# A two-layer decoder trunk: feed-forward up products all token-major, gated result transposed after, weights split 1024 columns at a time

## The chip, the cores and the metric

The kernel runs on one core of a Trainium2 chip. The metric is the device time of one execution in microseconds (us). Engines are called as the profile calls them: PE (matrix products and transposes), DVE, ACT and POOL (elementwise work), SP (it only issues the big DMAs). Each engine runs its own instructions strictly in order.

## What is computed

Two layers of a decoder trunk on 256 tokens of width 1024. Layer 0 mixes tokens by multi-scale causal pooling, layer 1 by differential attention; both have a memory cross-attention beside the mixer and a half-step gated feed-forward network (FFN) before and after it, so there are four FFNs.

```python
def swiglu(h, w_up, w_down):
    gate, up = jnp.split(h @ w_up, 2, axis=-1)          # w_up 1024 x 5632, w_down 2816 x 1024
    return (jax.nn.silu(gate) * up) @ w_down
...
    mem_n = rmsnorm(mem, mem_norm_g)
    for i in range(DEPTH):                               # DEPTH = 2
        kv = mem_n @ mem_w_kv[i]
        x = x + 0.5 * swiglu(rmsnorm(x, norm_g[i, 0]), ffn_w_up[i, 0], ffn_w_down[i, 0])
        h = rmsnorm(x, norm_g[i, 1])
        mix = pool_layer(...) if i == 0 else diff_layer(...)   # on h, with keys and values from kv
        x = x + mix
        x = x + 0.5 * swiglu(rmsnorm(x, norm_g[i, 2]), ffn_w_up[i, 1], ffn_w_down[i, 1])
    return rmsnorm(x, final_norm_g)
```

## The kernel before

**Numbers in two parts.** Every operand of a product is held as the sum of two float32r tiles, `hi` and `lo`; a product is three matmuls (hi·hi, hi·lo, lo·hi, lines 231 to 233). Weights come as pieces of 128x2048 floats: SP loads a piece into one of three raw buffers (`RB`), ACT casts it to `hi` (L205), DVE subtracts to get `lo` (L208), in steps of `SPLIT` = 512 columns, into one of four pairs of buffers (`WB`). A raw buffer is free when its last `lo` is done. Operands made on the way are split the same way: a cast on ACT (`gh`, L220), then a subtraction on DVE (`gl`, L226).

**An FFN** works through 11 chunks of 256 hidden features (`ffn`, `NJ`). For a chunk it needs two pieces of up weights (gate and up columns) and one of down weights. After up product j the down product of an earlier chunk follows, which adds to four PSUM banks `acc`. Up products come in two forms. *Token-major* (`proj_tok`): the x columns are stationary and 512 weight columns move, 24 matmuls 128x512 per token tile t, two tiles. The gated result g then has tokens on partitions and is turned by PE transposes (L237, tile tr), 2 per token tile, cast to `gh` and subtracted to `gl`. *Feature-major* (`proj_wide`, L377, L379, L376): 128 weight columns are stationary, 8 matmuls of 512 and 8 of 256 columns per column tile, four column tiles a chunk; the result already lies as `gh` and `gl` need it, and `gate_columns` and `up_columns` do the rest on ACT and DVE. The first FFN does its first 3 chunks token-major, the others their first one; the other 38 chunks are feature-major. These need the norm's factor along the free axis, which `row_rstd` (L258) makes with four small matmuls (128x128 each in the profile), once per FFN.

**Closing a stage** (`close`): for a token tile, x is transposed in two halves of four transposes each, and for each half ACT makes four 128x128 `xT` hi parts with the gain (L222) and DVE four lo parts (L228), straight from PSUM.

**The order** of PE, ACT, DVE and SP is laid down while the program is built: `Flow` keeps a model clock, the products advance it, and chains of dependent steps (splitting a piece, gating a chunk, one attention head) are put between them when their model time comes. `finish` forces a chain's remaining steps in at once. `Weights` keeps the queue of pieces and issues a load as soon as a raw buffer counts as free. Special entries of the queue are `x` (its load goes to x itself, no raw buffer), `cols` and `mem` (the memory, split and normalised once, planned at j = 6 of the first FFN) and `final`. In the pool mixer `diff_consts` loads 64-wide constants `lp` by SP (L787), POOL multiplies them (`pr`), DVE sums (`dots`, L795), ACT takes exp (`ex`).

Of the kernel before, what the change touches and what calls it, by code (L numbers as in the profile page):

```python
# [35 lines left out]
SPLIT = 512  # L36
PACE = 0.0016
HURRY = 0.0016
AHEAD = 1
WB = 4  # L40
RB = 3
T2K = 8
ORDERED = {mybir.EngineType.PE, mybir.EngineType.Activation, mybir.EngineType.DVE, mybir.EngineType.SP}
# [7 lines left out]
# Spacing of the steps of a chain, in microseconds.  # L51
# [3 lines left out]
GATE = (1.1, 0.5, 0.25, 1.2, 0.05)  # L55
# [47 lines left out]
class Weights:  # L103
    """Pieces of the weights in the order of their use: loaded ahead, split ahead, handed out, released."""

    def __init__(self, flow, load, run):
        self.flow, self.load, self.run = flow, load, run
        self.queue, self.raw, self.done = [], [], {}
        self.started = self.live = 0
        self.running = False  # L110

    def pump(self):
        while len(self.raw) < min(len(self.queue), self.started + RB):
            self.raw.append(self.load(*self.queue[len(self.raw)]))
        if self.running or self.started == len(self.queue):
            return
        if isinstance(self.queue[self.started][0], tuple):
            if self.live == WB:
                return
            self.live += 1  # L120
        self.running = True
        self.flow.add(self.next())

    def next(self):
        key, src = self.queue[self.started]
        self.done[key] = yield from self.run(key, self.raw[self.started])
        self.started += 1
        self.running = False
        self.pump()
# [12 lines left out]
def trunk(ctx, tc, I, out):  # L142
# [8 lines left out]
    ps_tr = ctx.enter_context(tc.tile_pool(name="ps_tr", bufs=2, space=PSUM))  # L151
# [14 lines left out]

    def tr_bank():
        return ps_tr.tile([P, 512], F32, tag="tr", name=nm("tr"))

    def raw_tile():  # L170
        return wp.tile([P, PIECE], F32, tag="raw", name=nm("raw"), bufs=RB)

# [13 lines left out]
    def load(key, src):  # L186
# [4 lines left out]
        raw = raw_tile()  # L191
# [4 lines left out]
    def split_piece(key, raw):  # L196
# [5 lines left out]
        for s in range(0, PIECE + SPLIT, SPLIT):  # L202
            if s < PIECE:
                sl = slice(s, s + SPLIT)
                nc.scalar.copy(hi[:, sl], raw[:, sl])  # L205
            if s:
                sl = slice(s - SPLIT, s)
                nc.vector.tensor_sub(lo[:, sl], raw[:, sl], hi[:, sl].bitcast(F32))  # L208
            yield (PACE if len(W.done) >= AHEAD else HURRY) * SPLIT
        return hi, lo  # L210

    W = Weights(F, load, split_piece)
# [17 lines left out]
    def mm3(o, lh, ll, rh, rl, start, stop):  # L230
        nc.tensor.matmul(o, lh, rh, start=start, stop=False)  # L231
        nc.tensor.matmul(o, lh, rl, start=False, stop=False)  # L232
        nc.tensor.matmul(o, ll, rh, start=False, stop=stop)  # L233
# [20 lines left out]
    def row_rstd(rstd):  # L254
        """rstd of the tokens, along the free axis of every partition."""
# [20 lines left out]
    def columns(name):  # L276
        """Feature-major operand, K tile by K tile: both parts, and the two side by side."""
# [15 lines left out]
    def close(t, gain0):  # L293
# [6 lines left out]
        def parts(h):  # L300
            for k in range(4 * h, 4 * h + 4):
                yield xT[0][:, k, cols(t)], xT[1][:, k, cols(t)], b[h][:, cols(k % 4)], gcol[:, gain0 + k:gain0 + k + 1]

        def hi(h):
            for th, tl, src, g in parts(h):
                split_hi(th, src, g)

        def lo(h):
            for th, tl, src, g in parts(h):
                split_lo(tl, th, src, g)  # L310
# [4 lines left out]
        hi(0)  # L315
# [4 lines left out]
        hi(1)  # L320
# [23 lines left out]
    def proj_tok(hx, pcs, t, bank=mm_bank):  # L344
        """[128 tokens, 512] = h @ w; w in two pieces of four K tiles."""
# [11 lines left out]
    def proj_feat(hx, pcs, c):  # L357
        """[128 features, 256 tokens] for column tile c of the pieces."""
# [9 lines left out]
    def proj_wide(hx, pcs, c):  # L368
        """The same as two halves of a bank, to be added: the weights' first part meets both parts at once."""
        F.finish(*ready)  # L370
        o = mm_bank()
        for kk in range(KT):
            wh, wl = [v[:, kk % 4, cols(c)] for v in pcs[kk // 4]]
            last = kk == KT - 1
            if last:
                nc.tensor.matmul(o[:, 0:SEQ], wl, hx[0][:, kk, :], start=False, stop=False)  # L376
            nc.tensor.matmul(o, wh, hx[2][:, kk, :], start=kk == 0, stop=last)  # L377
            if not last:
                nc.tensor.matmul(o[:, 0:SEQ], wl, hx[0][:, kk, :], start=False, stop=False)  # L379
# [669 lines left out]
```

## Time and profile before

| | |
|---|---|
| time, median of 3 runs | 1035.28 us (1034.5 to 1036.14) |
| span of the profiled execution | 1033.5 us |
| PE busy | 1022.4 us, 99% of the span |
| DVE busy | 739.6 us, 72% |
| ACT busy | 610.4 us, 59% |
| weights and inputs read | 186.3 MB, 181 GB/s over the span |
| one raw piece, issue to landing | 4.8 us (median, up weights) |

The page gives the busy time of each engine, the span in 40 slices and the chain of work that ended last. The span runs from the first to the last profiled instruction; the median time is 1.8 us above it.

### The profile page before, as it was taken

What the parts mean: (1) busy time and instruction counts of PE and PEld (TensorE: products, weight loads), DVE (VectorE), ACT (ScalarE), POOL (GpSimd) and SP (SyncE); (2) the same over time, 40 slices, a digit from 0 to 9 for tenths busy, and PEclk for the clock granted to TensorE, in tenths of its full rate; (3) what the DMA queues carried; (4) which work ended last, traced back from release to release, by engine and by line L of the source; (5) the groups of instructions that cost most, each with busy time, mean ns of one, the idle gap of its engine ahead of it and who ended that gap; (6) DMA issues with size and microseconds to landing.
All of it is one profiled execution on the core that took longest, in us unless ns stands there. A gap on an engine that the chain in (4) does not pass through costs nothing.

```text
span 1033.5 us, 15028 instructions
## 1 busy us (share of the span) xinstructions
PE 1022.4 (99%) x5624; PEld 882.0 (85%) x5624; DVE 739.6 (72%) x1533; ACT 610.4 (59%) x1357; POOL 55.8 (5%) x125
## 2 busy tenths in 40 slices
PE   8999999999999999999999999999999999999997
PEld 7888888899888888888888888889998888888886
DVE  5767887756767677777777777756877867777675
ACT  5655755765666555556655565654766666555553
POOL 0000520100000000000000000010211000000000
PEclk9999999999999999999999999999999999999999
DMA  8754745535544555544554545446334544455541
GB/s 300 286 189 163 267 181 204 201 130 188 182 140 168 192 199 193 200 170 163 204 202 165 204 163 204 169 157 237 120 134 142 185 158 168 164 203 178 195 178 41
DMA packets 27993, 188.31 MB, mean 182 GB/s; under 512 B 3216, under 2 KB 3472, under 8 KB 5904
## 3 DMA queue, kind: packets, MB, share of 16 engines
q1 hardware_dynamic: 27632, 186.82, 49.7%
q8 instruction: 44, 0.72, 0.3%
q10 hardware_dynamic: 288, 0.52, 0.1%
q14 instruction: 29, 0.24, 0.1%
HBM read 186.29 MB, written 1.05 MB: 181 GB/s over the span
## 4 chain that ended last, share of the span: by engine, by line
PE 95%; DVE 2%; ACT 1%; DMA 1%; POOL 0%; SPq 0%; issue 0%; POOLq 0%; ACTq 0%
PE mm L377 28%; PE mm L379 12%; PE acc L231 10%; PE acc L233 10%; PE acc L232 10%; PE mm L231 6%; PE mm L233 6%; PE mm L232 6%; PE mm L376 2%; PE tr L237 1%; DMA raw<-in_ffn_w_up 1%; DVE lo L208 1%; ACT ds L841 1%; PE acc L822 0%; PE tr L232 0%; PE tr L233 0%
## 5 line engine op out<-in xcount | busy, mean ns | idle before, releaser
L208 DVE TENSOR_TENSOR lo<-raw,hi 128x512 fp32r<-128x512 f32 x684 | 440.7, 688 | 43.0 <-ACT hi L205 42.7
L377 PE MATMUL mm<-xT,hi 128*128 128x512 f32 x1216 | 424.2, 398 | 0.0
L205 ACT CAST hi<-raw 128x512 fp32r<-128x512 f32 x684 | 385.1, 618 | 26.9 <-PE mm L232 14.2
L379 PE MATMUL mm<-xT,lo 128*128 128x256 f32 x1064 | 298.5, 281 | 0.0
L377 PEld LDWEIGHTS mm<-xT,hi 128*128 128x128 f32 x1216 | 220.8, 188 | 42.4
L379 PEld LDWEIGHTS mm<-xT,lo 128*128 128x128 f32 x1064 | 201.0, 189 | 6.4
L231 PE MATMUL acc<-hi,gh 128*128 128x512 f32 x352 | 138.1, 392 | 0.0
L233 PE MATMUL acc<-hi,gl 128*128 128x512 f32 x352 | 137.1, 389 | 0.0
L232 PE MATMUL acc<-lo,gh 128*128 128x512 f32 x352 | 137.0, 389 | 0.0
L385 DVE TENSOR_TENSOR g<-g,mm 128x256 f32<-128x256 f32 x76 | 32.0, 421 | 80.6 <-ACT g L384 80.4
L384 ACT COPY s<-mm 128x256 f32<-128x256 f32 x76 | 28.3, 372 | 98.7 <-PE mm L377 98.7
L232 PEld LDWEIGHTS acc<-lo,gh 128*128 128x128 f32 x352 | 66.2, 188 | 13.9
L233 PEld LDWEIGHTS acc<-hi,gl 128*128 128x128 f32 x352 | 66.1, 188 | 14.0
L231 PEld LDWEIGHTS acc<-hi,gh 128*128 128x128 f32 x352 | 66.1, 188 | 11.9
L385 DVE TENSOR_TENSOR s<-s,mm 128x256 f32<-128x256 f32 x76 | 31.9, 420 | 57.8 <-ACT s L384 57.7
L439 ACT ACTIVATE s<-s 128x256 f32<-128x256 f32 x76 | 31.8, 418 | 68.5 <-DVE s L437 68.5
L220 ACT CAST gh<-g 128x256 fp32r<-128x256 f32 x76 | 30.9, 407 | 65.8 <-DVE g L445 65.8
L231 PE MATMUL mm<-xT,hi 128*128 128x256 f32 x192 | 55.9, 291 | 0.0
L233 PE MATMUL mm<-xT,lo 128*128 128x256 f32 x192 | 54.5, 284 | 0.0
L232 PE MATMUL mm<-xT,hi 128*128 128x256 f32 x192 | 54.3, 283 | 0.0
L231 PE MATMUL mm<-hi,xT 128*128 128x512 f32 x128 | 50.9, 398 | 0.0
L233 PE MATMUL mm<-hi,xT 128*128 128x512 f32 x128 | 50.0, 390 | 0.0
(190 smaller groups left out, 1364.1 us busy)
## 6 DMA issues: line engine op xcount, KB each, us to landing
raw<-in_ffn_w_up SPq DMA_DIRECT2D x86, 1024.0 KB, 4.8
raw<-in_ffn_w_down SPq DMA_DIRECT2D x44, 1024.0 KB, 5.0
raw<-in_diff_w_in SPq DMA_DIRECT2D x14, 1024.0 KB, 4.8
raw<-in_mem_w_kv SPq DMA_DIRECT2D x8, 1024.0 KB, 4.8
raw<-in_pool_w_in SPq DMA_DIRECT2D x6, 1024.0 KB, 4.9
raw<-in_pool_w_out SPq DMA_DIRECT2D x6, 1024.0 KB, 4.8
raw<-in_diff_w_out SPq DMA_DIRECT2D x6, 1024.0 KB, 4.7
raw<-in_ffn_w_up SPq DMA_DIRECT2D x8, 256.0 KB, 7.0
```

Source lines behind the costliest of these rows:

```text
L205: nc.scalar.copy(hi[:, sl], raw[:, sl])
L208: nc.vector.tensor_sub(lo[:, sl], raw[:, sl], hi[:, sl].bitcast(F32))
L220: nc.scalar.copy(hi, src)
L231: nc.tensor.matmul(o, lh, rh, start=start, stop=False)
L232: nc.tensor.matmul(o, lh, rl, start=False, stop=False)
L233: nc.tensor.matmul(o, ll, rh, start=False, stop=stop)
L376: nc.tensor.matmul(o[:, 0:SEQ], wl, hx[0][:, kk, :], start=False, stop=False)
L377: nc.tensor.matmul(o, wh, hx[2][:, kk, :], start=kk == 0, stop=last)
L379: nc.tensor.matmul(o[:, 0:SEQ], wl, hx[0][:, kk, :], start=False, stop=False)
L384: nc.scalar.copy(out, o[:, SEQ:2 * SEQ])
L385: nc.vector.tensor_add(out, out, o[:, 0:SEQ])
L439: nc.scalar.activation(s, s, AF.Silu)
```

## The change

1. `proj_wide`, `gate_columns`, `up_columns` and `row_rstd` inside the FFN are gone. Every chunk is token-major (`single`). The four transposes of a chunk stand together, after the second token tile's gating, in one bank (`one_bank("tr")`, a single buffer); `gh` and `gl` are then one 128x512 operation each. With `steps`, the down product lags one chunk (two in the first FFN), and the last step holds the last two (three) down products.
2. `SPLIT` is 1024: a piece is two casts on ACT, then two subtractions on DVE.
3. `close` copies each PSUM tile with its gain to SBUF (`xc`, four ACT operations per half as before), then casts all four 128x128 tiles in one ACT operation and subtracts in one DVE operation.
4. `Weights` counts free buffers by tag. The entry `x` takes no raw buffer but gives one back, so the count of free raw buffers is one too high from there on, and loads stand one piece earlier in SP's order.
5. `plan_ffn` adds `cols` and `mem` when `js[-1] == 5`, which holds for the up step and for the down step of chunk 5: the memory is loaded, split and normalised twice.
6. Further buffers' tags, `gh` and `gl` with three buffers; queries and keys in one tile.

```diff
-SPLIT = 512
-PACE = 0.0016
-HURRY = 0.0016
+SPLIT = 1024
+PACE = 1.2
+HURRY = 0.8
...
+        key, _, _, pre, post, frees = self.queue[self.started]
...
+        for tag in frees:
+            self.free[tag] += 1
...
         for s in range(0, PIECE, SPLIT):
+            nc.scalar.copy(hi[:, sl], raw[:, sl])
+            yield pace
+        for s in range(0, PIECE, SPLIT):
+            nc.vector.tensor_sub(lo[:, sl], raw[:, sl], hi[:, sl].bitcast(F32))
...
+        def scaled(h):
+            c = t2k("xc").rearrange("p (k n) -> p k n", k=4)
+            for k in range(4):
+                g = gain0 + 4 * h + k
+                nc.scalar.activation(c[:, k, :], b[h][:, cols(k)], AF.Copy, scale=gcol[:, g:g + 1])
+            b[h] = c
+            split_hi(xT[0][:, 4 * h:4 * h + 4, cols(t)], c)
 
         def lo(h):
-            for th, tl, src, g in parts(h):
-                split_lo(tl, th, src, g)
+            split_lo(xT[1][:, 4 * h:4 * h + 4, cols(t)], xT[0][:, 4 * h:4 * h + 4, cols(t)], b[h])
...
+            gts[j, t] = g
+            if t == 0:
+                return
+            yield SLACK
+            if begin and j in HOLD:
                 yield max(0, HOLD[j] - F.now)
+            F.finish(other)
+            part_tiles(j)
+            b = one_bank("tr")
+            for i in range(NT):
+                transposes(b[:, cols2(i)], gts[j, i], 2)
...
+        def single(j):
+            pcs = pieces(*[(layer, f, "up", j, q) for q in range(2)])
+            for t in range(NT):
+                o = proj_tok(xT, pcs, t, acc_bank if begin and j == 2 else mm_bank)
+                ids[j, t] = F.add(gated(j, t, o, ids.get((j, 0))))
+            ids[j, 0] = ids[j, 1]
             W.release(2)
...
+    def steps(begin):
+        lag = 2 if begin else 1
+        order = [("single", j) for j in range(lag - 1, lag)]
+        for j in range(lag, NJ):
+            order += [("single", j), ("down", j - lag)]
+        return order[:-1] + [("down", *range(NJ - 1 - lag, NJ))]
...
+            if begin and kind == "single" and js[0] == 2:
+                W.add("x", I["x"].rearrange("b (t p) d -> p (b t) d", p=P), "none")
+            if begin and js[-1] == 5:
+                W.add("cols", I["mem_cols"])
+                W.add("mem", I["mem"].rearrange("b (t p) d -> p (b t) d", p=P))
```

**Place one: the first FFN's start.** DVE, while the first three chunks are gated, before (acc and mm are products, tr the transposed chunks, rstd the norm's factor):

```order
L208 TENSOR_TENSOR lo_364<-raw_275,hi_363 128x512 x4
L416 SCALAR_TENSOR_TENSOR g_388<-acc_349,rstd_317,s_387 128x256
L208 TENSOR_TENSOR lo_402<-raw_311,hi_401 128x512 x2
L226 TENSOR_TENSOR gl_101<-tr_412,gh_100 128x512
L208 TENSOR_TENSOR lo_402<-raw_311,hi_401 128x512 x2
L226 TENSOR_TENSOR gl_253<-tr_432,gh_252 128x512
L260 COPY row_453<-tr_450 128x256
```

and now:

```order
L248 TENSOR_TENSOR lo_331<-raw_214,hi_330 128x1024 x2
L442 SCALAR_TENSOR_TENSOR g_370<-acc_333,rstd_276,s_375 128x256
L248 TENSOR_TENSOR lo_361<-raw_240,hi_360 128x1024 x2
L267 TENSOR_TENSOR gl_389<-tr_390,gh_388 128x512
L267 TENSOR_TENSOR gl_410<-tr_411,gh_409 128x512
L442 SCALAR_TENSOR_TENSOR g_421<-acc_371,rstd_292,s_432 128x256
```

Both `gl` of the first two chunks now follow two pairs of `lo` directly, and the transposes that the second one reads (tr_411) go into the same bank as the first one's (tr_390); before they had two banks.

**Place two: the pool mixer.** SP's order of loads before:

```order
L193 DMA raw_2008<-in_mem_w_kv 128x2048
L193 DMA raw_2098<-in_pool_w_in 128x2048
L787 DMA lp<-in_diff_lambda 128x256
L193 DMA raw_2148<-in_pool_w_in 128x2048
L193 DMA raw_2215<-in_mem_w_kv 128x2048
L193 DMA raw_2286<-in_mem_w_kv 128x2048
```

and now:

```order
L230 DMA raw_1684<-in_pool_w_in 128x2048
L230 DMA raw_1766<-in_pool_w_in 128x2048
L230 DMA raw_1795<-in_mem_w_kv 128x2048
L807 DMA lp<-in_diff_lambda 128x256
L230 DMA raw_1850<-in_mem_w_kv 128x2048
```

With three buffers in turn, a load takes over the buffer of the third load before it: the load ahead of `lp`, raw_2098, that of the pool groups' weights; now raw_1795 that of raw_1632. DVE at the same place, before (cat_lo are results of pool groups, pl their operands):

```order
L208 TENSOR_TENSOR lo_2153<-raw_2008,hi_2152 128x512
L226 TENSOR_TENSOR pl_2169<-acc_2170,ph_2168 128x512
L208 TENSOR_TENSOR lo_2153<-raw_2008,hi_2152 128x512 x2
L795 TENSOR_REDUCE dots<-pr 128x2
L226 TENSOR_TENSOR pl_2193<-acc_2194,ph_2192 128x512
L208 TENSOR_TENSOR lo_2223<-raw_2098,hi_2222 128x512 x2
```

and now:

```order
L269 SCALAR_TENSOR_TENSOR cat_lo_1615<-tr_1822,gcol,cat_hi_1614 128x256 x2
L267 TENSOR_TENSOR pl_1836<-acc_1837,ph_1835 128x512
L248 TENSOR_TENSOR lo_1799<-raw_1632,hi_1798 128x1024
L815 TENSOR_REDUCE dots<-pr 128x2
L267 TENSOR_TENSOR pl_1866<-acc_1867,ph_1865 128x512
L248 TENSOR_TENSOR lo_1863<-raw_1684,hi_1862 128x1024
```

Now the last reader of raw_1632, the second half of lo_1799, is the instruction just before `dots`, and `dots` needs `lp` by way of POOL; pl_1866, the operand of the last pool group, stands behind `dots`.

**Place three: the end of an FFN.** DVE at the end of the second FFN, before (x_res<-acc is the stage's result):

```order
L385 TENSOR_TENSOR s_4592<-s_4592,mm_4594 128x256
L437 TENSOR_TENSOR s_4592<-s_4592,row_3135 128x256
L385 TENSOR_TENSOR g_4593<-g_4593,mm_4624 128x256
L444 TENSOR_TENSOR g_4593<-g_4593,row_3135 128x256
L445 TENSOR_TENSOR g_4593<-g_4593,s_4592 128x256
L208 TENSOR_TENSOR lo_4646<-raw_4528,hi_4645 128x512
L226 TENSOR_TENSOR gl_4537<-g_4593,gh_4536 128x256
L208 TENSOR_TENSOR lo_4646<-raw_4528,hi_4645 128x512 x3
L291 SCALAR_TENSOR_TENSOR x_res<-acc_3258,x_res 128x512
```

and now:

```order
L267 TENSOR_TENSOR gl_3799<-tr_3800,gh_3798 128x512
L248 TENSOR_TENSOR lo_3790<-raw_3672,hi_3789 128x1024 x2
L442 SCALAR_TENSOR_TENSOR g_3815<-mm_3772,rstd_2604,s_3820 128x256
L442 SCALAR_TENSOR_TENSOR g_3847<-mm_3816,rstd_2693,s_3854 128x256
L248 TENSOR_TENSOR lo_3849<-raw_3708,hi_3848 128x1024 x2
L248 TENSOR_TENSOR lo_3872<-raw_3760,hi_3871 128x1024 x2
L267 TENSOR_TENSOR gl_3880<-tr_3881,gh_3879 128x512
L333 SCALAR_TENSOR_TENSOR x_res<-acc_2812,x_res 128x512
```

All four 1024-wide subtractions of the next two pieces now stand between the last chunk's g and its gl. PE there, before:

```order
L231 MATMUL acc_3259<-hi_4530,gh_4382 128x512
L232 MATMUL acc_3259<-lo_4531,gh_4382 128x512
L233 MATMUL acc_3259<-hi_4530,gl_4383 128x512
L231 MATMUL acc_3258<-hi_4573,gh_4536 128x512
L232 MATMUL acc_3258<-lo_4574,gh_4536 128x512
L233 MATMUL acc_3258<-hi_4573,gl_4537 128x512
```

and now:

```order
L273 MATMUL acc_2813<-hi_3762,gh_3798 128x512
L274 MATMUL acc_2813<-lo_3763,gh_3798 128x512
L275 MATMUL acc_2813<-hi_3762,gl_3799 128x512
L279 MATMUL tr_3881<-ident,g_3815 128x128 x2
L279 MATMUL tr_3881<-ident,g_3847 128x128 x2
L273 MATMUL acc_2812<-hi_3789,gh_3879 128x512
L274 MATMUL acc_2812<-lo_3790,gh_3879 128x512
L275 MATMUL acc_2812<-hi_3789,gl_3880 128x512
```

The last chunk's four transposes stand between the down product of the chunk before it and its own, whose first matmuls read gh_3879 and gl_3880; before, nothing stood there.

## Rows read from the trace of the kernel before

**Rows 1.** The page: engines' busy us (share, instructions); the last-ending chain by engine
```profile
PE 1022.4 (99%) x5624; PEld 882.0 (85%) x5624; DVE 739.6 (72%) x1533; ACT 610.4 (59%) x1357; POOL 55.8 (5%) x125
...
PE 95%; DVE 2%; ACT 1%; DMA 1%; POOL 0%; SPq 0%; issue 0%; POOLq 0%; ACTq 0%
```

**Rows 2.** By windows: us, five engines' busy (instructions), granted PEclk, DMA share, GB/s
```profile
340.64:357.36 16.72, 16.72 (x90) 14.32 (x89) 12.15 (x25) 9.47 (x20) 0.00 (x0) 1.00 0.51 190
...
1026.70:1030.00 3.30, 0.00 (x0) 0.00 (x0) 1.87 (x4) 1.51 (x4) 1.00 (x3) 1.00 0.00 0
1030.00:1031.00 1.00, 0.00 (x0) 0.00 (x0) 0.00 (x0) 0.03 (x1) 0.00 (x0) 0.52 0.33 121
```

**Rows 3.** Waits of PE: us in total, times, longest us
```profile
PE tr L237 <- DVE on L876: 1.2, 3, 0.6
```

**Rows 4.** Chain of waits, first FFN in steady state: start us, us, what
```profile
57.21 0.47 PE mm L377 x2
60.03 0.47 PE mm L377 x2
...
73.93 0.47 PE mm L377 x2
```

**Rows 5.** PE's timeline, pool mixer into second FFN: start us, us, what
```profile
304.06 0.39 PE L231 MATMUL mm<-hi,xT 128*128 128x512 f32 x1
...
308.14 0.60 PE L237 MATMUL tr<-ident,x_res 128*128 128x128 f32 x4
...
309.97 0.60 PE L237 MATMUL tr<-ident,x_res 128*128 128x128 f32 x4
310.33 0.48 PE L231 MATMUL mm<-hi,xT 128*128 128x512 f32 x1
```

**Rows 6.** Group by form: work, count | busy us, mean ns | idle
```profile
L237 PE MATMUL tr<-ident,x_res 128*128 128x128 f32 x80 | 12.0, 272 | 0.0
```

**Rows 7.** Timeline of ACT, DVE and PE, first FFN, chunks being gated
```profile
39.59 0.59 ACT L220 CAST gh<-tr 128x512 fp32r<-128x512 f32 x1 [1.29 <-PE tr L237]
...
37.80 0.48 DVE L416 SCALAR_TENSOR_TENSOR g<-acc,rstd,s 128x256 f32<-128x256 f32 x1
...
40.21 0.69 DVE L226 TENSOR_TENSOR gl<-tr,gh 128x512 fp32r<-128x512 f32 x1 [0.74 <-ACT gh L220]
...
41.46 0.60 PE L237 MATMUL tr<-ident,g 128*128 128x128 f32 x4
```

**Rows 8.** Timeline of SP, POOL, DVE and PE in the pool mixer
```profile
216.74 0.43 SPq L787 DMA_DIRECT2D lp<-in_diff_lambda  x1
...
221.52 0.65 POOL L793 TENSOR_TENSOR pr<-lp 128x64 f32<-128x64 f32 x2 [16.45 <-DMA lp<-in_diff_lambda]
...
226.41 1.28 DVE L208 TENSOR_TENSOR lo<-raw,hi 128x512 fp32r<-128x512 f32 x2
...
227.61 0.28 DVE L795 TENSOR_REDUCE dots<-pr 128x2 f32<-128x128 f32 x1
...
230.27 0.28 PE L231 MATMUL tr<-ph,hi 128*128 128x256 f32 x1
```

**Rows 9.** Timeline of ACT and DVE, pool mixer into second FFN, one closing half
```profile
308.78 1.14 ACT L222 ACTIVATE xT<-tr,gcol 128x128 fp32r<-128x128 f32 x4 [1.63 <-PE tr L237]
...
309.96 1.13 DVE L228 SCALAR_TENSOR_TENSOR xT<-tr,gcol,xT 128x128 fp32r<-128x128 f32 x4 [0.91 <-ACT xT L222]
```

**Rows 10.** Timeline of ACT, DVE and PE, end of the third FFN
```profile
664.74 0.40 PE L231 MATMUL acc<-hi,gh 128*128 128x512 f32 x1
...
665.33 1.28 ACT L398 ACT_TABLE_LOAD   x1
...
667.68 0.42 DVE L226 TENSOR_TENSOR gl<-g,gh 128x256 fp32r<-128x256 f32 x1 [0.39 <-ACT gh L220]
```

**Rows 11.** PE's timeline at the start: start us, us, work, idle before
```profile
6.43 0.80 PE L231 MATMUL acc<-hi,xT 128*128 128x512 f32 x1 [1.54 <-ACT xT L222]
...
9.59 0.40 PE L232 MATMUL acc<-lo,xT 128*128 128x512 f32 x1
```

More of the change, by code (lines that the diff above doesn't have):

```diff
@@ L124, in next @@
     def next(self):
-        key, src = self.queue[self.started]
-        self.done[key] = yield from self.run(key, self.raw[self.started])
+        key, _, _, pre, post, frees = self.queue[self.started]
+        raw, before = pre(self.raw) if pre else (self.raw.get(key), None)
+        self.done[key] = yield from self.run(key, raw, before)
+        if post:
+            yield from post(self.raw)
+        for tag in frees:
+            self.free[tag] += 1
         self.started += 1
@@ L194, in load, with split_piece @@
         return raw
-    def split_piece(key, raw):
+    def split_piece(key, raw, before):
         if not isinstance(key, tuple):
@@ L201, in split_piece @@
         lo = wp.tile([P, PIECE], F32R, tag="lo", name=nm("lo"))
[L202 to L209, printed above, removed]
+        pace = PACE if len(W.done) >= AHEAD else HURRY
+        for s in range(0, PIECE, SPLIT):
+            sl = slice(s, s + SPLIT)
+            if before is not None:
+                nc.vector.tensor_add(raw[:, sl], raw[:, sl], before[:, sl])
+            nc.scalar.copy(hi[:, sl], raw[:, sl])
+            yield pace
+        for s in range(0, PIECE, SPLIT):
+            sl = slice(s, s + SPLIT)
+            nc.vector.tensor_sub(lo[:, sl], raw[:, sl], hi[:, sl].bitcast(F32))
+            if s + SPLIT < PIECE:
+                yield pace
         return hi, lo
-    W = Weights(F, load, split_piece)
+    W = Weights(F, load, split_piece, {"raw": RB, "qk": 1, "mq": 1, "none": 1})
     special = {}
@@ L314, in close @@
         yield CLOSE[1]
-        hi(0)
+        scaled(0)
         yield CLOSE[2]
@@ L319, in close @@
         lo(0)
-        hi(1)
+        scaled(1)
         yield CLOSE[4]
@@ L366, in proj_feat @@
         return o
[L368 to L379, printed above, removed]
-            F.spend(0.325)
-        return o
-    def add_halves(out, o):
-        nc.scalar.copy(out, o[:, SEQ:2 * SEQ])
-        nc.vector.tensor_add(out, out, o[:, 0:SEQ])
     def accumulate(acc, t, lh, ll, pc, k0, first, end=None):
@@ new lines, in downs @@
+        def downs(*js):
+            if not acc and js:
+                acc.extend([acc_bank() for _ in range(2)] for _ in range(NT))
+            for i in js:
+                wds[i] = W.get((layer, f, "down", i), 2)
+                for t in range(NT):
+                    down(i, t)
+                W.release(1)
+        def single(j):
+            pcs = pieces(*[(layer, f, "up", j, q) for q in range(2)])
+            for t in range(NT):
+                o = proj_tok(xT, pcs, t, acc_bank if begin and j == 2 else mm_bank)
+                ids[j, t] = F.add(gated(j, t, o, ids.get((j, 0))))
+            ids[j, 0] = ids[j, 1]
+            W.release(2)
@@ new lines, in ffn @@
+        if begin:
+            for t, o in enumerate(begin()):
+                ids[0, t] = F.add(gated(0, t, o, ids.get((0, 0))))
+            ids[0, 0] = ids[0, 1]
+        for kind, *js in steps(begin):
+            if kind == "single":
+                single(*js)
+            elif NJ - 1 not in js:
+                downs(*js)
+            else:
+                if exp_next:
+                    F.add(exp_table(), EXP_AT)
+                for t in range(NT):
+                    for i in js:
+                        if t == 0:
+                            wds[i] = W.get((layer, f, "down", i), 2)
+                        down(i, t, end if i == NJ - 1 else None)
+                        if t == 1:
+                            W.release(1)
@@ L904, in diff_mix @@
         for i in range(2):
-            qs = group(i, 0)
-            ks = group(i, 2)
+            both = act.tile([P, 2, 4, SEQ], F32, tag="qk", name=nm("qk"), bufs=ROOM["qk"])
+            qs = group(i, 0, both[:, 0])
+            ks = group(i, 2, both[:, 1])
             for h in range(4):
@@ L968, in trunk @@
     plan_in("pool", 1)
-    W.queue.append((("pool", "group"), I["pool_w_group"]))
+    W.add(("pool", "group"), I["pool_w_group"])
     plan_mem(0, 0)
```

242 lines of the change are left out of this document (101 added, 141 removed).

## The prediction

> **What bounds the kernel now.** I read the page first: the engines' busy time and the chain that ended last. PE is busy for 1022.4 of 1033.5 us and carries 95% of the chain [rows 1]; DVE has 72%, ACT 59%. Then the table by windows for one steady chunk: of its 16.72 us PE works 16.72, DVE 12.15, ACT 9.47, at the full clock [rows 2]. Of PE's waits, what remains inside the program is 1.2 us in the diff mixer [rows 3]. So this kernel is a row of PE instructions without holes: a change is worth what it takes out of that row, less the holes it tears. Relief of DVE and ACT is worth nothing while PE is full; what counts on them is only the order, where PE comes to wait for a last subtraction.
>
> **1. The steady chunk, 38 times: +2.6.** A feature-major column tile takes 57.21 to 60.03, 2.82 us; four are 11.28, and a chunk has 16.72 from 57.21 to 73.93 [rows 4]. The rest, 5.44, is 24 down matmuls. A token-major product runs 18 matmuls from 304.06 to 308.14, 0.2267 each [rows 5]; 48 of them are 10.88. That saves 0.40 a chunk. But the gated result must now be transposed by PE: from the group of four transposes at 308.14 to the next at 309.97 are 1.83 us, in which six matmuls have 1.36, so a group puts the stream back by 0.47 [rows 5]. Net +0.07 a chunk. Ends: 0.36, from the group at 309.97 to the matmul behind it at 310.33 [rows 5], gives -1.6 for all; the mean length of a single transpose, 0.272 [rows 6], if nothing overlapped, gives 1.09 a group and +26. I take 0.47, since it is what a group did to just such a stream. The gating itself lies beside the down product. By 128x512 rows DVE would have two g at 0.48, one gl at 0.69 [rows 7] and six 1024-wide lo, together 8.4 of 16.8 us, ACT less: both are lighter than now.
>
> The Trainium skill (TensorE: Matmul & The Clock Gate, Part 4: PE-mode transpose) gives about 275 ns for a transpose within a kernel, which is the length in the trace but not the delay. Taken as a delay it would make 1.10 a group and some 24 us more in all; no row here shows a group holding its stream so long.
>
> **2. Work that goes, and one that comes twice: -1.4.** Four row_rstd, one per FFN, each four 128x128 matmuls, priced as a group of transposes: 4 x 0.47 = -1.9. The memory's statistics are done twice, one such group more: +0.5. The second memory's two pieces and its 16 operations go into the room that DVE and ACT gain in a chunk (12.15 against 8.4); without that cover each 128x256 operation would cost its 0.42 [rows 10]. The pairs of transposes in the six chunks that were token-major already become groups of four: nothing.
>
> **Price of a 1024-wide operation.** No row shows one on DVE. A subtraction of 256 columns takes 0.42 [rows 10], of 512 0.69 [rows 7]; on the same line 1024 give 1.22. Two neighbours of 512 take 1.28 [rows 8], 0.10 less than their sum, so in a queue I reckon 1.13 (estimate). Ends: 0.69 if the length hardly counted, 1.28 if nothing were saved.
>
> **3. Start, one bank for the transposed chunks: +1.1 (0 to 1.3).** PE turns the second chunk at 41.46 [rows 7]. It now waits for the first chunk's gl, whose queue on DVE is g, two 1024-wide lo, gl. ACT's casts ahead of the third s are twice as long, so I put the end of this g near 39.6 (now 37.80 + 0.48 [rows 7]); with 2 x 1.13 and 0.69 gl ends at 42.5, 1.1 late. Behind the waiting transposes stand only products, which all move.
>
> **4. Pool mixer, the load of lp behind a blocked queue: +4.5 (0 to 6).** Now lp is issued at 216.74, POOL has it at 221.52 and works 0.65, and dots at 227.61 finds it long done [rows 8]. In the new order SP must first wait for the half lo that ends right before dots, about where it ends now, 227.2 to 227.7 (226.41 + 1.28 [rows 8]). From there: issue of the raw load 0.4 (as lp's), 4.78 to POOL's start, 0.65, dots 0.28 [rows 8], and pl, as long as gl, 0.69 [rows 7]: 6.8 us, so 234.0 to 234.5. All of DVE stands behind dots, and the last pool group's product, which reads that pl, is due at 230.27 [rows 8]. PE waits 3.7 to 4.2, I take 4.1, and 0.4 for the memory product behind it, whose bank DVE also frees late. Zero holds only if PE were that far behind DVE here.
>
> **5. Closing with one operation for four: +1.9 (1.5 to 2.4).** ACT's four scaled copies end at 308.78 + 1.14 = 309.92 [rows 9]. In the present order DVE's four lo follow at once, from 309.96 [rows 9]; in the new one a 128x512 cast (0.59) and a subtraction (0.69) [rows 7] follow one another: hi at 310.5, lo at 311.2. The next product starts at 310.33 [rows 5], and its third matmul, 0.45 later, reads lo: 0.5 late, up to 0.8 with the second half. This holds where that product starts directly behind its own closing: the three entries into the second, third and fourth FFN. At the two entries into mixers two products lie between, 10.9 us, and hide it.
>
> **6. The ends of the four FFNs: +9.2 (4.8 to 10.4).** Before, the last gl (667.68 + 0.42) was there when the first down matmuls of the stage's end, from 664.74, had run [rows 10]. Now PE runs one token tile of the chunk before (12 matmuls, 2.72), transposes, and needs gh for the next matmul and gl for the third. Let E be the end of the last product; unhindered, the third matmul would start at E + 2.72 + 0.36 + 0.45 = E + 3.53.
> - Last FFN, no pieces left on DVE: transposes end at E + 3.32, gh 0.59, gl 0.69 [rows 7], hence E + 4.7: +1.2.
> - First FFN: two tiles stand ahead, so the transposes come late and the chain is as bare: +1.2.
> - Second FFN: g ends at E + 1.25 (s and g 0.48 each [rows 7], hand-overs), then four lo of 1.13, then gl: E + 6.5: +3.0.
> - Third FFN: ACT also loads its exp table, 1.28 [rows 10], ahead of the casts on which those lo wait: gl ends near E + 7.3: +3.8.
>
> The low end is 1.2 for all four, if DVE got its pieces done earlier; the high end has 1.28 for a lo.
>
> **7. Diff mixer: 0 (-1.2 to +3).** Its instructions interleave differently. What PE waits there now, 1.2 [rows 3], may go; a head's step may also find a 1024-wide operation in front, 0.5 longer than now, some six times in a row of dependent steps. I take neither.
>
> **Sum.** 2.6 - 1.4 + 1.1 + 4.5 + 1.9 + 9.2 = 17.9. The span of 1033.5 becomes 1051.4; the median lies 1.8 above the span of the profiled execution, so 1053. A measurement can tell about 0.2%, 2 us, from no change.
>
> **The rivals.**
> - *The holes are half covered.* PE is behind DVE at the pool group, and the ends cost only their bare chains: 17.9 - 4.5 - 4.4 = 9.0, 1044 us. For it: DVE gains 3.7 us per chunk and may be further ahead. Against it: the g that starts the queue at an FFN's end can't come before the product's end. 14%.
> - *The clock falls in the new holes.* After PE's end the granted clock stayed 1.00 over 3.3 idle us and was 0.52 in the next one [rows 2]: half of it, the lower of its two levels. The hole in the pool mixer (4.1) and that of the third FFN (3.8) are longer. At the start seven matmuls took 3.16 us [rows 11] for 1.59 at full pitch: 1.6 lost per fall. One or two falls, with 7 at its upper end: 1056 to 1059. 13%.
> - *Faster: the transposes run in the shadow of the matmuls.* If a group put the stream back by 0.10 instead of 0.47, 38 chunks would give -11.4, and with the holes at their low ends (0 + 0 + 1.5 + 4.8) and -1.4 the sum is -6.5: 1029. With these holes it turns faster by 2 us below 0.22 a group. For it: PE's weight loads overlap its matmuls (85% busy beside 99% [rows 1]). Against it: no group in the rows costs less than 0.36. 5%.
> - *No difference.* All costs at their low ends give +2: 1037; a little less and nothing shows. 4%.
> - *A transpose costs its length* (the page's rule under 1): 1.09 a group from rows 6, +23.6: 1077. 2%.
>
> **Chances.** The forecast, 1047 to 1059, has 62%. The range 1041 to 1062 leaves out the last three rivals, the low tail of the first and the high ends of several costs at once, some 20%. Faster 5%, same 4%, slower 91%.
>
> **What would show it.** Chunk period 16.8 us where it was 16.72; a PE wait of about 4 us on pl beside a DVE wait of about 6 us on dots; PE waits on gl of 1 to 4 us at the end of each FFN and of half a microsecond at the three entries; row_rstd gone from the FFNs. It is wrong if the chunk's period falls below 16.6, if dots doesn't wait, or if PE's waits sum to under 8 us.

## The result, and the profile after

The changed kernel took 1060.89 us (median of 4 runs, 1059.55 to 1063.88) beside 1034.89 for the kernel before: a ratio of 1.0256, 95% interval 1.0239 to 1.0273. That is 26 us more; the forecast was 1053, 18 more, with 1047 to 1059 as the likely band and a range of 1041 to 1062. The profiled execution has a span of 1059.1 us, 25.6 more than before.

The page after, the engines' line and the engines of the chain that ended last, answering [rows 1]:

```profile
PE 1034.4 (98%) x5156; PEld 868.1 (82%) x5156; DVE 581.2 (55%) x794; ACT 540.9 (51%) x857; POOL 58.7 (6%) x129
...
PE 88%; DVE 4%; ACT 3%; DMA 2%; issue 1%; POOL 1%; SPq 0%; POOLq 0%; ACTq 0%; DVEq 0%
```

PE is busy for 12 us more, and idle for 13.6 us more. DVE works 158 us less than before (581 for 740) and ACT 70 less; none of that shows in the time. The waits of PE (us in total, times, longest), answering [rows 3]:

```profile
PE acc L273 <- ACT gh L261: 4.3, 4, 2.2
PE tr L274 <- DVE pl L267: 3.9, 1, 3.9
PE acc L275 <- DVE gl L267: 2.5, 2, 1.6
...
PE tr L279 <- DVE on L896: 1.6, 2, 1.4
PE mm L273 <- DVE mq L267: 1.1, 1, 1.1
```

Before, this list had one line beside those of the start, 1.2 us. Now the ends of the four feed-forwards stand there (gh, gl), the pool mixer (pl) and the diff mixer (on, mq).

The stages, read off PE's timelines as the start of the first product of each, show where the time came in (us; "step" is what the stretch ending there adds):

| first product of | before | after | later by | step |
|---|---|---|---|---|
| pool mixer | 195.09 | 196.73 | 1.64 | 1.64 |
| second FFN | 304.06 | 311.64 | 7.58 | 5.94 |
| third FFN | 490.31 | 503.40 | 13.09 | 5.51 |
| diff mixer | 676.57 | 697.08 | 20.51 | 7.42 |
| fourth FFN | 841.18 | 864.34 | 23.16 | 2.65 |
| (PE's last matmul) | 1026.27 | 1051.70 | 25.43 | 2.27 |

The steady chunk, answering [rows 4 and 5]: PE's timeline of the first FFN, the groups of transposes of the first two chunks, then of three chunks in a row with the matmul behind the first of them, and the next.

```profile
37.98 0.60 PE L279 MATMUL tr<-ident,g 128*128 128x128 f32 x4
...
40.74 0.66 PE L279 MATMUL tr<-ident,g 128*128 128x128 f32 x4
...
51.48 0.60 PE L279 MATMUL tr<-ident,g 128*128 128x128 f32 x4
51.84 0.48 PE L273 MATMUL mm<-hi,xT 128*128 128x512 f32 x1
...
68.29 0.60 PE L279 MATMUL tr<-ident,g 128*128 128x128 f32 x4
...
85.09 0.60 PE L279 MATMUL tr<-ident,g 128*128 128x128 f32 x4
...
102.80 0.60 PE L279 MATMUL tr<-ident,g 128*128 128x128 f32 x4
```

From 51.48 on are 16.81 and 16.80 us from group to group, where a chunk took 16.72 before. The next chunk takes 17.71: it holds the first of the two normalisations of the memory.

The pool mixer, answering [rows 8]: SP, POOL, DVE and PE.

```profile
229.30 0.33 SPq L230 DMA_DIRECT2D raw<-in_mem_w_kv  x1
229.68 0.43 SPq L807 DMA_DIRECT2D lp<-in_diff_lambda  x1
...
234.53 0.59 POOL L813 TENSOR_TENSOR pr<-lp 128x64 f32<-128x64 f32 x2 [26.56 <-DMA lp<-in_diff_lambda]
...
228.02 1.22 DVE L248 TENSOR_TENSOR lo<-raw,hi 128x1024 fp32r<-128x1024 f32 x1
235.16 0.28 DVE L815 TENSOR_REDUCE dots<-pr 128x2 f32<-128x128 f32 x1 [5.92 <-POOL pr L813]
235.36 0.68 DVE L267 TENSOR_TENSOR pl<-acc,ph 128x512 fp32r<-128x512 f32 x1
...
231.91 0.28 PE L273 MATMUL tr<-ph,hi 128*128 128x256 f32 x1
236.09 0.39 PE L274 MATMUL tr<-pl,hi 128*128 128x256 f32 x1 [3.91 <-DVE pl L267]
```

SP issues the raw load at 229.30, when the lo from 228.02 has ended, and lp behind it at 229.68; POOL begins at 234.53, dots at 235.16 after 5.92 us of waiting, and PE, which stopped behind the matmul at 231.91, goes on at 236.09. Beside the order shown at place two of the change, this is the forecast chain, link by link.

The end of the second FFN: DVE, ACT and PE. Below it PE at the ends of the third and of the last FFN.

```profile
487.36 0.48 DVE L442 SCALAR_TENSOR_TENSOR g<-mm,rstd,s 128x256 f32<-128x256 f32 x1 [3.37 <-ACT s L437]
487.76 4.62 DVE L248 TENSOR_TENSOR lo<-raw,hi 128x1024 fp32r<-128x1024 f32 x4
492.30 0.68 DVE L267 TENSOR_TENSOR gl<-tr,gh 128x512 fp32r<-128x512 f32 x1
...
490.06 0.58 ACT L261 CAST gh<-tr 128x512 fp32r<-128x512 f32 x1
...
489.38 0.60 PE L279 MATMUL tr<-ident,g 128*128 128x128 f32 x4
490.70 0.50 PE L273 MATMUL acc<-hi,gh 128*128 128x512 f32 x1 [0.72 <-ACT gh L261]
...
493.04 0.59 PE L275 MATMUL acc<-hi,gl 128*128 128x512 f32 x1 [1.61 <-DVE gl L267]
...
681.14 0.60 PE L279 MATMUL tr<-ident,g 128*128 128x128 f32 x4
683.97 0.50 PE L273 MATMUL acc<-hi,gh 128*128 128x512 f32 x1 [2.23 <-ACT gh L261]
...
685.73 0.80 PE L275 MATMUL acc<-hi,gl 128*128 128x512 f32 x1 [0.92 <-DVE gl L267]
...
1042.07 0.60 PE L279 MATMUL tr<-ident,g 128*128 128x128 f32 x4
...
1044.07 0.50 PE L275 MATMUL acc<-hi,gl 128*128 128x512 f32 x1
```

In the second FFN four 1024-wide lo stand between the last g and gl, from 487.76 on; gl starts at 492.30, 1.66 us after gh was ready, and the third matmul at 493.04.

What the forecast did not count is in the table by windows (as [rows 2], the clock is the figure ahead of the last two):

```profile
237.50:240.60 3.10, 3.10 (x16) 3.10 (x16) 3.01 (x6) 1.83 (x4) 0.00 (x0) 0.50 0.16 21
...
486.00:489.00 3.00, 3.00 (x15) 2.49 (x14) 1.64 (x3) 2.14 (x3) 0.00 (x0) 1.00 0.59 249
493.50:496.40 2.90, 2.90 (x8) 2.27 (x7) 0.69 (x1) 0.00 (x0) 0.00 (x0) 0.50 1.02 427
...
686.40:691.00 4.60, 4.60 (x12) 3.55 (x11) 1.29 (x2) 0.00 (x0) 0.00 (x0) 0.50 0.64 269
```

Behind three of the waits PE runs at 0.50, the lower of its two levels; at 486, ahead of the second wait, it has 1.00.

### The profile page after: what moved, and what is told of

Read it like the earlier page. It is cut to its first block, busy times and chain, and to the rows that moved or that the text cites. A ratio compares the mean times of both kernels' runs of the same rounds, so it can differ in the third digit from the quotient of the medians.

```text
span 1059.1 us, 12948 instructions
## 1 busy us (share of the span) xinstructions
PE 1034.4 (98%) x5156; PEld 868.1 (82%) x5156; DVE 581.2 (55%) x794; ACT 540.9 (51%) x857; POOL 58.7 (6%) x129
## 4 chain that ended last, share of the span: by engine, by line
PE 88%; DVE 4%; ACT 3%; DMA 2%; issue 1%; POOL 1%; SPq 0%; POOLq 0%; ACTq 0%; DVEq 0%
PE mm L273 18%; PE mm L275 18%; PE mm L274 18%; PE acc L275 10%; PE acc L273 9%; PE acc L274 9%; PE tr L279 3%; DVE lo L248 2%; ACT hi L244 1%; DMA raw<-in_ffn_w_up 1%; DMA raw<-in_ffn_w_down 0%; DMA lp<-in_diff_lambda 0%; ACT ds L861 0%; PE acc L842 0%; PE tr L687 0%
## 5 line engine op out<-in xcount | busy, mean ns | idle before, releaser
L244 ACT CAST hi<-raw 128x1024 fp32r<-128x1024 f32 x342 | 342.1, 1048 | 178.1 <-PE mm L275 78.8
L248 DVE TENSOR_TENSOR lo<-raw,hi 128x1024 fp32r<-128x1024 f32 x342 | 402.0, 1221 | 28.3 <-ACT hi L244 27.9
L273 PE MATMUL mm<-hi,xT 128*128 128x512 f32 x736 | 291.5, 396 | 0.2
L275 PE MATMUL mm<-hi,xT 128*128 128x512 f32 x736 | 287.5, 391 | 0.0
L274 PE MATMUL mm<-lo,xT 128*128 128x512 f32 x736 | 286.8, 390 | 0.0
L275 PEld LDWEIGHTS mm<-hi,xT 128*128 128x128 f32 x736 | 138.1, 188 | 30.5 <-DVE xT L267 1.3
L273 PEld LDWEIGHTS mm<-hi,xT 128*128 128x128 f32 x736 | 138.2, 188 | 27.9 <-ACT xT L261 0.9
L274 PEld LDWEIGHTS mm<-lo,xT 128*128 128x128 f32 x736 | 138.4, 188 | 27.6 <-DVE lo L248 0.3
L267 DVE TENSOR_TENSOR gl<-tr,gh 128x512 fp32r<-128x512 f32 x44 | 30.4, 691 | 180.8 <-ACT gh L261 180.7
L442 DVE SCALAR_TENSOR_TENSOR g<-mm,rstd,s 128x256 f32<-128x256 f32 x84 | 40.4, 481 | 135.3 <-ACT s L437 135.3
L437 ACT ACTIVATE s<-mm,rstd 128x256 f32<-128x256 f32 x84 | 39.9, 475 | 95.1 <-PE mm L275 95.0
L275 PE MATMUL mm<-xT,lo 128*128 128x256 f32 x192 | 54.5, 284 | 0.2 <-DVE lo L248 0.2
```

The source lines that it names most:

```text
L267: nc.vector.tensor_sub(lo, src, hi.bitcast(F32))
L273: nc.tensor.matmul(o, lh, rh, start=start, stop=False, skip_group_check=more)
L274: nc.tensor.matmul(o, lh, rl, start=False, stop=False, skip_group_check=more)
L275: nc.tensor.matmul(o, ll, rh, start=False, stop=stop, skip_group_check=more)
L437: nc.scalar.activation(s, o[:, 0:FC], AF.Silu, scale=rstd[t])
L442: nc.vector.scalar_tensor_tensor(dst, o[:, FC:2 * FC], rstd[t], s, op0=ALU.mult, op1=ALU.mult)
```

## The experiments

Each starts from the changed kernel unless said otherwise. All times are medians beside runs of the kernel before on the same chip (1034.81 to 1035.08).

**x gives back no buffer.** The count of free raw buffers is then right, and lp stands behind a load whose buffer is free.

```diff
-                W.add("x", I["x"].rearrange("b (t p) d -> p (b t) d", p=P), "none")
+                W.add("x", I["x"].rearrange("b (t p) d -> p (b t) d", p=P), "none",
+                      frees=("none",))
```

> The changed kernel, with the entry x giving back no raw buffer, so that loads stand one piece later in SP's order and lp is issued behind a load whose buffer is free. Theory (a hole on pl of 3.9 us, then about 2 us of half clock behind it): the wait of PE on pl and the wait of DVE on dots disappear, and with them the stretch of half clock; 1060.9 - 6 = about 1055 us. Rival (the pool mixer is slower because of the 1024-wide pieces, and another wait takes the place of the one on pl): the mixer's stretch stays within 1 us of 115 us, about 1060.

Measured 1053.74 us, ratio 1.0183 (1.0168 to 1.0198): 7.2 under the changed kernel. The pool mixer's stretch gives 5.68 of it. The table by windows: the pool mixer, and the stretches behind the ends of the second and the third FFN.

```profile
228.00:236.00 8.00, 8.00 (x69) 8.00 (x68) 6.37 (x12) 4.75 (x10) 2.07 (x4) 1.00 0.53 184
486.80:489.80 3.00, 3.00 (x14) 2.41 (x14) 1.18 (x2) 0.00 (x0) 0.00 (x0) 1.00 1.01 423
678.50:683.50 5.00, 5.00 (x13) 3.79 (x12) 1.38 (x2) 0.00 (x0) 0.00 (x0) 0.50 0.61 254
```

PE no longer waits in the pool mixer (8.00 of 8.00 us busy) and keeps its clock. The second FFN's end was a surprise: the wait there is as long as in the changed kernel, but the clock stayed at 1.00 behind it, which gave 1.6 us more.

**lp by another queue.** To part lp from the other loads, which all stand elsewhere in the first experiment, here only lp's queue is changed.

```diff
-        nc.sync.dma_start(lp, I["diff_lambda"].to_broadcast([P, 4, 64]))
+        nc.scalar.dma_start(lp, I["diff_lambda"].to_broadcast([P, 4, 64]))
```

> The changed kernel, with the small load of lp issued by ACT instead of SP and nothing else changed. Theory (lp stands behind a load that waits for a buffer): PE's wait on pl falls from 3.9 to under 1 us and the half clock behind it goes: 1060.9 - 5.5 = about 1055.4, all of it between the start of the pool mixer and the start of the second feed-forward. Rival (lp is late for another reason, or DVE is late there in any case): 1059 or more.

Measured 1055.28 us, ratio 1.0196 (1.0180 to 1.0211): 5.6 less. The pool mixer's stretch is 5.65 shorter and no other stretch moves by more than 0.4. So the place of lp behind a blocked load makes 5.65 of the 5.94 us that this stretch had gained: a wait of 4.1, the half clock of 1.4 behind it, and little else.

**The last chunk gated without delay.**

```diff
-            yield SLACK
+            yield SLACK if j < NJ - 1 else 0
```

> The changed kernel, with the last chunk of each feed-forward gated without the delay before its transposes, so that its gl stands behind one half lo on DVE instead of four. Theory (the four ends cost 8.5 us of waits and, at two of them, 4.3 us of half clock behind the wait): the waits shrink to about half a microsecond each, the clock stays at its full level there; 1060.9 - 11 = about 1050 us. Rival 1 (the pieces now pushed behind the last gl are late for the next stage): the waits reappear at the entries, under 4 us gained, about 1057. Rival 2 (the half clock has nothing to do with the waits): it stays, 1060.9 - 7 = 1054.

Measured 1050.57 us, ratio 1.0152 (1.0137 to 1.0167): 10.3 less, as expected. The stretches that end the four FFNs are shorter by 1.17, 3.92, 5.48 and 0.67, and nothing of it is given back at the entries behind. DVE at the end of the second FFN:

```profile
486.34 1.22 DVE L248 TENSOR_TENSOR lo<-raw,hi 128x1024 fp32r<-128x1024 f32 x1
488.53 0.69 DVE L267 TENSOR_TENSOR gl<-tr,gh 128x512 fp32r<-128x512 f32 x1 [0.97 <-ACT gh L261]
```

One lo stands ahead of gl, which now waits only for gh. The clock stays at 1.00 there and at the end of the third FFN (677.0 to 682.0 in this profile), where the changed kernel had 0.50, so rival 2 falls too.

**Pieces in 512 columns again.**

```diff
-SPLIT = 1024
-PACE = 1.2
-HURRY = 0.8
+SPLIT = 512
+PACE = 0.6
+HURRY = 0.4
```

> The changed kernel, with pieces split in 512 columns as before, the model's pace halved with it. Theory (what counts is the order, not the width): the ends stay within 0.5 us of what they are (eight subtractions of 0.6 in place of four of 1.13) with their half clock; the diff mixer gives back most of its 2.65 us; lp comes behind a load whose buffer was freed earlier, so the 6 us of the pool mixer go; about 1052. Rival (the 1024-wide pieces themselves make the waits): the waits at the ends of the second and third feed-forward fall by more than half and their half clock with them, about 1043.

Measured 1054.75 us, ratio 1.0194 (1.0179 to 1.0209): 6.1 less. The theory is right in kind, though it had 2.7 more: the pool mixer gives 4.12 (lp's load stands behind a free buffer in this order), the diff mixer 1.77, and the ends stay in kind. The second FFN's stretch is 0.3 longer; the third's is 1.3 shorter, more than expected, with a wait almost as long (3.02 for 3.15) and fewer matmuls at half clock behind it. DVE at the end of the second FFN:

```profile
483.91 4.89 DVE L248 TENSOR_TENSOR lo<-raw,hi 128x512 fp32r<-128x512 f32 x8
488.72 0.68 DVE L267 TENSOR_TENSOR gl<-tr,gh 128x512 fp32r<-128x512 f32 x1
```

Eight lo of 512 columns take 4.89 us ahead of gl, four of 1024 took 4.62. The width is not what makes the waits there.

**Filled holes.** Is it the idling that brings the clock down?

```diff
+FILL = 20
...
             F.finish(ids[j, t])
+            if j == NJ - 1 and t == 0 and (layer, f) in ((0, 1), (1, 0)):
+                wb = one_bank("tr2")
+                for _ in range(FILL):
+                    nc.tensor.matmul(wb[:, 0:P], ident, ident, start=True, stop=True)
             accumulate(acc, t, *gts[j], wds[j], 0, j == 0, end)
```

> The changed kernel, with 20 matmuls 128x128 of the identity with itself (into a bank that nobody reads) between the last chunk's transposes and its down product, in the second and third feed-forward; they take about 2.4 us of the 3.7 and 4.6 us that PE has there, so that its next matmul is not delayed. Theory (the clock falls because PE is idle in the hole): the 1.7 and 2.6 us of half clock behind the two waits go, about 1056.5. Rival (these small matmuls don't count, or the clock falls for another reason): no change, 1061.

Measured 1059.85 us, ratio 1.0244 (1.0227 to 1.0261). The expectation had the filling too short: it took 4.4 us in place of 2.4 (at each place the trace has 40 instructions of 128x128 for the 20 matmuls of the program), longer than the hole, and so cost time itself. The time therefore decides little; the clock does. The table by windows, the stretches behind the two fillings:

```profile
495.20:498.00 2.80, 2.80 (x15) 2.32 (x14) 0.69 (x1) 0.00 (x0) 0.00 (x0) 1.00 0.90 369
687.00:691.00 4.00, 4.00 (x23) 3.32 (x22) 1.38 (x2) 0.00 (x0) 0.00 (x0) 1.00 0.92 369
```

At both places the clock is 1.00, where the changed kernel had 0.50. At the second FFN's end that alone says little, since the clock also stayed up there in a profile with nothing filled (x gives back no buffer). At the third it fell in every other profile that has the wait, and the stretch is 1.88 us shorter in spite of the longer filling.

**The same program again.** Since the clock had stayed up once behind the same wait, the changed kernel was profiled a second time.

> The changed kernel once more, for its clock: in its first profile the clock fell behind three waits of PE (3.9 us in the pool mixer, 2.8 at the end of the second feed-forward, 3.8 at the end of the third), in the kernel whose x gives no buffer only behind the third although the second wait was as long. Theory (the same wait sometimes brings a fall and sometimes not): the three waits come back to within 0.1 us, the falls behind them need not; 1059 to 1063. Rival (the fall follows from the wait alone): all three again.

Measured 1061.01 us, ratio 1.0256 (1.0235 to 1.0278). The waits came back to within 0.1 us; the stretches behind the second and the third by windows:

```profile
494.00:497.00 3.00, 3.00 (x14) 2.43 (x15) 1.20 (x2) 0.00 (x0) 0.00 (x0) 1.00 1.00 415
685.70:690.70 5.00, 5.00 (x13) 3.78 (x12) 1.38 (x2) 0.00 (x0) 0.00 (x0) 0.50 0.62 247
```

No fall at the second FFN's end this time. Five profiles have this wait at its full length, with one or the other edit elsewhere: the clock fell behind it in three (the changed kernel, lp by another queue, transposes twice) and stayed in two (this one, x gives back no buffer). Behind the longer waits, in the pool mixer and at the third FFN's end, it fell in each of these five that has them.

**Every group of transposes twice** in chunks 2 to 9, 32 groups more.

```diff
-            for i in range(NT):
+            for i in (0, 1) * (1 if j in (0, 1, NJ - 1) else 2):
                 transposes(b[:, cols2(i)], gts[j, i], 2)
```

> The changed kernel, with the group of four transposes of a chunk done twice into the same place, in chunks 2 to 9 of each feed-forward (32 groups more). Theory (a group holds the stream of matmuls for 0.47 us, as one did before): 32 x 0.47 = +15 us, 1076. Rival 1 (a transpose costs its whole length of 0.27 us): 32 x 1.1 = +35, 1096. Rival 2 (transposes run in the shadow of the matmuls, 0.1 a group): +3, 1064.

Measured 1073.33 us, ratio 1.0369 (1.0354 to 1.0385): 12.4 more, 0.39 a group. PE's timeline, a double group and the matmul behind it:

```profile
365.37 1.03 PE L279 MATMUL tr<-ident,g 128*128 128x128 f32 x8
366.16 0.48 PE L273 MATMUL mm<-hi,xT 128*128 128x512 f32 x1
```

0.79 us from the group's start to the matmul, where a single group has 0.36. A group's price lies near 0.4 to 0.47; neither 0.1 nor 1.1 is near.

**Width alone, in the kernel before:** `SPLIT = 1024`, nothing else. (The model's pace counts by columns there, so a step's pace grows with it.)

> The kernel before, with pieces split in steps of 1024 columns and nothing else changed. Theory (the width hardly matters where gl doesn't stand behind whole pieces): only the diff mixer loses, up to its 2.65 us of the changed kernel: 1035 to 1038. Rival (coarse pieces alone make the waits of the changed kernel): several us at each end of a feed-forward, 1043 or more.

Measured 1045.79 us, ratio 1.0106 (1.0091 to 1.0121): 11 us slower, and my expectation was wrong, the rival's number right. Not in its places, however: the second and third FFN add 1.1 each, while the first adds 4.8, the pool mixer 1.5, the diff mixer 2.3. PE's waits in that kernel:

```profile
PE tr L237 <- DVE on L876: 2.3, 2, 1.2
PE acc L231 <- ACT gh L220: 1.4, 3, 0.9
...
PE mm L232 <- DVE lo L208: 1.1, 2, 0.6
...
PE acc L233 <- DVE gl L226: 0.6, 1, 0.6
```

Many small waits at over a dozen places, on gh, gl, lo, on and x. A wide operation takes 1.22 us where a narrow one takes 0.69, so one that lands in front of an awaited operation can cost some 0.5 more; how much of the 11 us is this, and how much the order laid anew for wide steps, is not parted. So width by itself is not harmless: whether it costs depends on the order around it. The changed kernel has another order and other places; there the width costs what the 512 run gives back without lp, little beyond the diff mixer.

**Three repairs at once:** x gives back nothing, the last chunk without delay, and the memory planned once. The first two edits stand above; the third:

```diff
-            if begin and js[-1] == 5:
+            if begin and kind == "down" and js[-1] == 5:
```

> The changed kernel with three repairs: x gives back no raw buffer, the last chunk is gated without delay, the memory is planned once. Theory (the holes add up): 1060.9, less 7.1 and 10.3 as each repair gave alone, 1.6 of half clock that both had taken away counted back, less 0.6 for the second memory: about 1044.5. Rival (the holes cover one another, so that one opens where another closes): 1048 or more.

Measured 1043.6 us, ratio 1.0081 (1.0066 to 1.0096): 0.9 under the sum of the parts, no more than the runs of one kernel spread. The holes add up.

**The old closing besides.** `scaled` and `lo` as before, 128x128 by 128x128 from PSUM.

```diff
-            c = t2k("xc").rearrange("p (k n) -> p k n", k=4)
...
-            split_hi(xT[0][:, 4 * h:4 * h + 4, cols(t)], c)
+            for th, tl, src, g in parts(h):
+                split_hi(th, src, g)
...
-            split_lo(xT[1][:, 4 * h:4 * h + 4, cols(t)], xT[0][:, 4 * h:4 * h + 4, cols(t)], b[h])
+            for th, tl, src, g in parts(h):
+                split_lo(tl, th, src, g)
```

> The three repairs and, besides, the closing of the kernel before (four casts and four subtractions of 128x128 straight from PSUM). Theory (the closing with one cast and one subtraction delays the first product of three stages by 0.3 us each, and no more): 0.5 to 1.5 us under the kernel with three repairs. Rival (the closing as forecast, 0.5 to 0.8 each and its lo late in the second half too): 2 us or more under it.

Measured 1041.45 us, ratio 1.0059 (1.0042 to 1.0076): 2.15 less, and the rival, the price as forecast, is right. In the profiles the stretches that hold an entry into the second, third and fourth FFN are 0.63, 0.61 and 0.62 shorter. I had lowered the price to 0.3 after reading only the first of the late matmuls. PE's timeline with the new closing (the kernel with three repairs), where the second FFN begins its product of the second token tile:

```profile
311.26 0.60 PE L279 MATMUL tr<-ident,x_res 128*128 128x128 f32 x4
311.91 0.50 PE L273 MATMUL mm<-hi,xT 128*128 128x512 f32 x1
312.25 0.40 PE L274 MATMUL mm<-lo,xT 128*128 128x512 f32 x1
312.64 0.50 PE L275 MATMUL mm<-hi,xT 128*128 128x512 f32 x1
312.98 0.39 PE L273 MATMUL mm<-hi,xT 128*128 128x512 f32 x1
```

From the transposes to the first matmul are 0.65 where [rows 5] has 0.36; the third starts 0.39 behind the second, where the pitch is 0.23, and the fourth 0.34: 0.29, 0.16 and 0.11.

**And 512 columns again with all this.** Of the change the token-major chunks and their order are left, and the smaller edits that no run here takes back (point 6 of the change, all casts of a piece ahead of its subtractions).

> The three repairs, the old closing and pieces split in 512 columns; of the change remain the token-major chunks and the order of the down products. Theory (the diff mixer's loss comes from 1024-wide pieces in front of a head's steps, 2.7 us; the chunks cost 0.08 each): 1041.5 - 2.5 = about 1039. Rival 1 (the diff mixer loses by its other interleaving): 1041. Rival 2 (all narrow, the token-major chunks are worth something after all): 1035 or less.

Measured 1040.87 us, ratio 1.0061 (1.0044 to 1.0077). By its time this is rival 1's number; the 0.6 us to the run before lie within the spread of the two. In the profile the diff mixer is 1.86 shorter, as the theory had it, but the third FFN's end takes 0.6 back, with a wait of 0.9 on gh, and the pool mixer 0.65. What stays above the kernel before is about 1 us in each of the two mixers and in each of the last three FFNs, 1.9 in the third. No version of these beats the kernel before.

## Why the prediction was right, point by point

The direction was right and the time lies in the range, near its upper end. It lies above the band of 1047 to 1059 that had 62%: the range held because it reached up to the falls of the clock, which the sum itself had at nothing. The holes stood where they were forecast, and nearly as long. By the steps of the prediction:

| term | forecast | measured | read from |
|---|---|---|---|
| 1 steady chunk, 38 times | +2.6 | +3.0 | period 16.80 for 16.72, times 38 |
| 2 row_rstd, memory twice | -1.9 + 0.5 | memory +0.9; row_rstd not parted | 85.09 to 102.80, 17.71 for 16.80 |
| 3 one bank at the start | +1.1 | +0.3 | second group 2.76 behind the first, for 2.50 |
| 4 lp | +4.5 | +4.1 | 231.91 to 236.09, less the usual 0.12 |
| 5 closings | +1.9 | +1.9 | 0.63, 0.61, 0.62 |
| 6 ends of the FFNs | +9.2 | +9.0 | 1.2, 2.9, 3.8, 1.2 |
| 7 diff mixer | 0 | +2.65 | its stretch |
| half clock | 0 (a rival) | +5.0 | 1.4, 1.4 and 2.2 behind three waits |

Point 6 was walked by hand through an order without times: 1.2, 3.0, 3.8, 1.2 were forecast for the four ends. From the start of the last chunk's transposes to the matmul that reads gl they measure, above the forecast's unhindered 0.81, 3.66 - 0.81 = 2.85 in the second FFN (489.38 to 493.04 above), 4.59 - 0.81 = 3.78 in the third (681.14 to 685.73), and 2.00 - 0.81 = 1.19 in the last (1042.07 to 1044.07) and in the first. In the third most of it shows as a wait on gh, 2.23, since ACT's table load (1.28 from 679.11 on) and three casts (2.92) stand ahead of gh, which starts at 683.34, as well as of the lo ahead of gl. Of the memory's 0.9, 0.35 is a wait of its transposes for gl (86.69 to 87.27, less the usual 0.23): they go into the same single bank.

**What failed.** The sum missed 8 us, by two steps.
- "Half clock": the rival "the clock falls in the new holes" was not an alternative to the forecast but came on top of it. It was put at 13% and at one or two falls of 1.6 each; the trace has three falls, of 1.4, 1.4 and 2.2 (the matmuls at the doubled pitch, 15 of 256 columns and 7 and 11 of 512, less their usual time). The prediction had the hole of the second FFN, 3.0, outside: the kernel before had shown 1.00 over 3.3 idle us. That row showed one such pause, and did not bound the others.
- "Diff mixer: 0 (-1.2 to +3). I take neither": its upper end was nearly right. PE's waits there grew from 1.2 [rows 3] to 2.7 (on and mq), and with 512 columns the mixer gave back 1.77 in one order and 1.86 in another. So some two thirds belong to the 1024-wide operations; what the rest is, isn't settled.

At the start (term 3) the sign was right and the size too big: g was ready sooner than reckoned (it ends at 37.81, for the 39.6 of the forecast). In the other profiles with 1024-wide pieces and this start the second group stands 2.51 to 3.19 behind the first, so the term is 0 to 0.7 from one execution to the next.

The measured terms, with -1.9 + 0.9 for the second, make 25.0. PE's last matmul came 25.4 later, though in that profile PE also got its first operands 1.4 earlier, of which a lead of 1.0 was left at the first group of transposes (37.98 for 38.96; kernels with the same start begin at 5.0 to 6.5 us, so this isn't the change's). Of the 1.4 us that are missing some 0.7 (estimate) are matmuls at the edges of the half clock, which the table leaves out: where no fall came, the second FFN's stretch is 1.6 shorter, for the table's 1.4. About 0.7 remain without a place of their own.

**The rivals.** "The holes are half covered" fell: both its parts, lp and the queue on DVE, came at nearly full price. "The transposes run in the shadow" and "a transpose costs its length" fell with the doubled groups, 0.39 each, and with the period. The Trainium skill's figure of some 275 ns for a transpose, given for bf16 (TensorE: Matmul & The Clock Gate, Part 4: PE-mode transpose), is near the length of one in this case's trace, 272 ns in f32. The page says nothing of what a stream pays for it: here four of them put a stream of matmuls back by 0.4 to 0.5 us and not by 1.1.

So the change bought nothing on the engine that sets the time: the token-major product saved 0.40 a chunk and its transposes took 0.47. What it saved, on DVE and ACT, was not wanted; and most of its further edits put a wait in front of PE.

## What to carry to other kernels

Where one engine is full, count an edit's instructions on that engine alone first; less work on the others buys nothing, but a longer or later operation of theirs in front of an awaited one costs what it holds that one up. In an order written ahead, look at the last item of each stage: little follows that could hide its chain, and what stands ahead of it in the queues of the other engines decides. A small load behind a big one that waits for a buffer waits with it, and all engines that read it do too.

## What the runs showed of the hardware that was not expected

PE's clock fell to half behind waits of 2.3 us in sum (0.72 and 1.61, with two matmuls between) up to 3.9; in the profiles with these waits at full length the matmuls at the whole doubled pitch took 2.1 to 5.1 us together and cost 1.0 to 2.4. Behind one and the same wait, that of 2.3 at the end of the second FFN, it fell in three profiles and not in two others; what decides it was not tried. When the waits at the ends of the second and third FFN were filled with small matmuls whose result nobody read, it did not fall there; at the third it fell in every profile with the wait unfilled. So a hole in this full PE often cost more than its length, and not the same in each execution.
